# Tuned hybrid SSD/MLP kernel: halves of h on VectorE up to tile 6, other rows for the scalings of x, two sums ahead of row 5's weights, one warm-up product less

## Chip, cores and metric

One core of one Trainium2 chip. The metric is the time of one execution on the device in microseconds (us), taken as the median of several runs. A measurement of this kernel tells changes apart from about 0.2% on. Where single instructions are spoken of, their times come from one execution that the hardware profiler recorded, counted from its first instruction.

The engines have the profile's names: PE is TensorE (matrix products; PEld is its weight loads), DVE is VectorE, ACT is ScalarE, POOL is GpSimd, SP is SyncE, which issues most DMAs. An engine works through its own instructions in order; a "q" behind its name (SPq) stands for its sequencer.

## The reference, cut to what matters

One layer of a generator: a modulated RMS norm, one wide projection, a state-space scan and a gated MLP side by side, and an output projection. The change touches how the modulated, normed input `h` is made and fed to the first columns of the projection.

```python
shift, scale, gate = jnp.split(sc @ w_ada[l] + b_ada[l], 3, axis=-1)          # sc = silu(c), 2048
shift_c, scale_c, gate_c = jnp.split(scc @ w_ada[l] + b_ada[l], 3, axis=-1)   # scc = silu(c_ctx)
hc = _rmsnorm(ctx, g_pre[l]) * (1.0 + scale_c) + shift_c                      # 256 context tokens
zc = hc @ (w_in[l][:, :XBC_W + DT_W] if last else w_in[l])
...
hx = _rmsnorm(x, g_pre[l]) * (1.0 + scale[:, None]) + shift[:, None]          # 256 latent tokens
zx = hx @ w_in[l]
...
x = x + gate[:, None] * out
```

All is float32. The model width is 2048, there are 256 latent and 256 context tokens and one layer.

## The kernel before

**Layout.** The width of 2048 is cut into 16 tiles of 128, one per partition; tile k of `xT` holds 128 channels by 512 tokens. Columns 0 to 255 of a tile are one token group, 256 to 511 the other (the latent tokens), and each has its own scale and shift, two columns of `hab`.

**Products in two parts.** A float32 factor is split into a rounded part (`hi`, `hhi`) and the rest (`lo`, `hlo`), and a product of two float32 tiles is three products on PE: hi by hhi, hi by hlo, lo by hhi. ScalarE rounds the weights (`split_hi`, L376), VectorE subtracts (`split_lo`, L384; `split_dt`, L380, for 64 columns of the step sizes).

**Making h.** For tile k:
- `scale_x` (VectorE, L387): x times g_pre times the tokens' 1/rms, one operation of 512 columns.
- scale and shift of the tile, into `hab`: from 1 MB chunks of w_ada. For tiles 0 to 3 PE alone forms the sums (L224, L253). From tile 4 on tiles go in pairs; PE sums over twelve of sixteen parts of c (`ada_mm`, L253), VectorE over the other four in eight operations of 512 columns (`ada_part`, L262: "the sums" in this text), and `ada_fin` (VectorE: L268, transpose L275, L278) puts both together.
- `make_h` (ScalarE, L394): x times scale plus shift, twice, once rounded into `hhi` and once in full into `xT`, each in two halves of 256 columns; four instructions.
- `make_hl` (VectorE, L398): `hlo` = `xT` - `hhi`.

**Rows.** The first stage goes through the 16 tiles; step kt of it, "row kt" here, multiplies tile kt of h with the first seven tiles and the step-size columns of w_in (`wst[kt]`, 480 KB). Each row begins on PE with `psdt` (L446), then L466 and L467 for three tiles, `psdt` with hlo, L469, then L143 to L145 for the rest. Each row also carries the making of the next tile of h, n = kt + 1, on the other engines, and PE's share (L224, L253) of the scale and shift of later tiles.

**What sets the order.** It is written out by hand: `row_steps(kt)` returns a list of steps, and each engine gets its instructions in that order (`tc.manual_schedule`). Letters are steps: c, d, l split the weights of row n, h makes h, e makes hlo, x scales a tile of x (which ones in row kt: `XROW`), v is one of VectorE's sums, b and f finish a pair of scale and shift, a is PE's share of them, m, p, q, w are the products of row kt. The loads are issued by SyncE in program order, two chunks of w_ada and one tile of weights per row, into six buffers of 1 MB and three of 480 KB. They go through one queue and land in that order.

Ahead of row 0 the squares of x are summed by PE for the 1/rms (L341), with products of no use between them (`warm`, L319) that keep PE busy; 512 and 256 are their columns.

After the rows, from about 130 us on, the kernel goes through the rest of w_in and w_out in tiles of 1 MB, with the scan between; the change does not touch that.

Of the kernel before, what the change touches and what calls it, by code (L numbers as in the profile page):

```python
# [11 lines left out]
AF = mybir.ActivationFunctionType  # L12
ALU = mybir.AluOpType
# [15 lines left out]
NSING = 4  # L29
KD = 12  # L30

XROW = ((3, 4, 5), (6, 7, 8), (9,), (10, 11), (12, 13), (14, 15))

LAST = (-1, 4, 5, 0, 1, 2, 3, 6)

# [12 lines left out]
def tile_hybrid_ssd_mlp(  # L48
# [19 lines left out]
    nc = tc.nc  # L68
# [61 lines left out]
    hab = stp.tile([P, KT, 2, 2], F32, name="hab")  # L130
# [7 lines left out]
    hhi = [hpool.tile([P, TOK], F32R, name=f"hhi{k}") for k in range(KT)]  # L138
# [8 lines left out]
    def bc(ap, axis, n):  # L147
        u = ap.unsqueeze(axis)
        shp = list(u.shape)
        shp[axis] = n  # L150
        return u.to_broadcast(shp)
# [4 lines left out]
    def yseg(j):  # L156
        return y[:, j // 4, (j % 4) * 512 : (j % 4 + 1) * 512]
# [6 lines left out]
    zt, e = yseg(5)[:, 0:256], yseg(5)[:, 256:512]  # L164
# [12 lines left out]
    xT = stx.tile([P, KT, TOK], F32, name="xT")  # L177
# [78 lines left out]
    def ada_part(u, i):  # L256

        q, v = divmod(i, 2)
        if i == 0:
            part[u] = ada_raw.pop(4 * u - 2 * NSING), st2.tile([P, 4, 2], F32, tag="part", name=f"part{u}")  # L260
        raw, acc = part[u]
        nc.vector.scalar_tensor_tensor(cbj, raw[:, q * 512 : (q + 1) * 512], 1.0, cb[v], op0=ALU.mult, op1=ALU.mult,  # L262
                                       accum_out=acc[:, q, v : v + 1])
# [6 lines left out]
    def ada_fin(u):  # L270

        ps = ada_ps.pop(u)
        n = 64 * len(UNITS[u])
        tr = st2.tile([P, 128], F32, tag="row", name=f"adat{u}")
        nc.vector.transpose(tr[:, 0:n], ps[:, 0:n])  # L275
        m = UNITS[u][0]
        b = part.pop(u)[1] if u in part else bc(bab[:, m], 2, 2)
        nc.vector.tensor_tensor(hab[:, m : m + n // 64].rearrange("p k q v -> p (k q) v"),  # L278
                                tr[:, 0:n].rearrange("p (q r) -> p q r", r=32)[:, :, 0:2], b, op=ALU.add)
# [37 lines left out]
    def warm(*ns):  # L317
        for n in ns:
            nc.tensor.matmul(psw[:, 0:n], lhsT=ones, rhs=ones[:, 0:1].to_broadcast([P, n]), start=True, stop=True)  # L319
# [12 lines left out]
    for k in range(KT):  # L332
        sq = sqs[k % 7]
        if k % 2:
            nc.vector.tensor_tensor(sq, xT[:, k, :], xT[:, k, :], op=ALU.mult)
        else:
            nc.scalar.activation(sq, xT[:, k, :], AF.Square)
            if k == 0:
                nc.scalar.copy(cb[1], pcv[1])
        g = k % 4  # L340
        nc.tensor.matmul(pss[32 * g : 32 * g + 32, :], lhsT=ones[:, 0:32], rhs=sq, start=k < 4, stop=k >= KT - 4)  # L341
        if g == 3:
            warm(512)
            if k < 12:
                warm(256)

# [25 lines left out]
    def split_hi(kt, a=0, b=WST):  # L372
        if a == 0:
            sp0[kt] = (wp["spl"].tile([P, WST + 64], F32R, tag="hi", name=f"hi_st{kt}"),
                       wp["spl"].tile([P, WST - 64], F32R, tag="lo", name=f"lo_st{kt}"))
        nc.scalar.copy(sp0[kt][0][:, 64 + a : 64 + b], wraw[kt][:, a:b])  # L376

    def split_dt(kt):
        hi = sp0[kt][0]
        nc.vector.tensor_tensor(hi[:, 0:64], wraw[kt][:, 0:64], hi[:, 64:P].bitcast(F32), op=ALU.subtract)  # L380
# [5 lines left out]
    def scale_x(kt):  # L386
        nc.vector.scalar_tensor_tensor(xT[:, kt, :], xT[:, kt, :], pc[:, C_GPRE + kt : C_GPRE + kt + 1], rb,  # L387
                                       op0=ALU.mult, op1=ALU.mult)

    def make_h(kt):  # L390
        sl = (slice(256, 512), slice(0, 256))
        for t in (hhi[kt], xT[:, kt, :]):
            for v, s in enumerate(sl):
                nc.scalar.activation(t[:, s], xT[:, kt, s], AF.Identity, bias=hab[:, kt, 1, v : v + 1],  # L394
                                     scale=hab[:, kt, 0, v : v + 1])

    def make_hl(kt):
        nc.vector.tensor_tensor(hlo[kt], xT[:, kt, :], hhi[kt].bitcast(F32), op=ALU.subtract)  # L398

# [8 lines left out]
    def row_steps(kt):  # L408


        m = [("m", i) for i in range(-1, NST)]
        if kt == KT - 1:
            out_ = [("m", i) for i in LAST]
            out_.insert(3, ("t", 0))
            for i in range(2):
                out_.insert(out_.index(("m", 4 + i)) + 1, ("z", i))
            return out_
        n = kt + 1
        c_, d_, l_, h_, e_ = [(w, n) for w in ("c", "d", "l", "h", "e")]
        m0 = [("m", -1), ("p", 0), ("p", 1), ("p", 2), ("w", 0), ("q", 0), ("q", 1), ("q", 2)]  # L420
        m1 = [("m", i) for i in range(3, NST)]
        u = (n - NSING) // 2 + NSING
        x = [("x", k) for k in XROW[kt]] if kt < len(XROW) else []
        p = 4 * u - 2 * NSING
        if n < NSING:
            r = [("r", 2 * n), ("r", 2 * n + 1)]
            q = 8 if n == 1 else 6
            v = [("v", (NSING, i)) for i in range(4)] if n == NSING - 1 else []
            return (m0[:q] + r + [c_, ("k", n), d_, ("l1", n)] + m1[:1] + [("g", n), ("o", n), h_, ("l2", n)] + (v[:2] or x[:1])
                    + [e_] + v[2:] + (x if v else x[1:]) + m0[q:] + m1[1:])  # L430
        if kt % 2 == 0:
            v = [("v", (u + 1, i)) for i in range(4)] if n + 1 < KT else []
            return [e_, c_, d_, l_] + v + x + m0 + m1
        v = [("v", (u, i)) for i in range(4, 8)] + [("b", u)]
        a = [("a", c) for c in range(p + 1, p + 4)]
        t = v + [("f", u), h_, d_, l_, e_] + x + [("h", n + 1)]
        if n == NSING:
            return m0[:5] + a[:2] + m0[5:] + m1[:1] + a[2:] + [c_] + t + m1[1:]
        return a[:1] + m0 + a[1:] + [c_] + t + m1

    STEPS = {"a": ada_mm, "f": ada_fin, "v": lambda ui: ada_part(*ui), "b": ada_bias, "r": ada_rows, "x": scale_x, "e": make_hl, "k": ada_keep, "g": ada_sum, "o": ada_one,
             "h": make_h, "c": split_hi, "d": split_dt, "l": split_lo,
             "l1": lambda n: split_lo(n, 64, WH), "l2": lambda n: split_lo(n, WH)}

# [4 lines left out]
    def step(kt, what, i):  # L449
        if what in STEPS:  # L450
            STEPS[what](i)
        elif what == "z":
# [21 lines left out]

    split_hi(0, 0, WH)
    scale_x(0)
    ada_fin(0)
    split_dt(0)
    make_h(0)
    split_lo(0, 64, WH)  # L480
    make_hl(0)
    split_hi(0, WH)
    split_lo(0, WH)
# [469 lines left out]
    for n, i in enumerate(REST):  # L953
        lat = ORDER[i] >= 24
        ps = acp.tile([P, 256 if lat else 512], F32, tag="acc", name=f"psx{i}")
        for hf in range(2):
            whi, wlo = half(2 * n + hf)
            for kk in range(8):
                k = 8 * hf + kk
# [164 lines left out]
    for blk in range(16):  # L1124
# [11 lines left out]
        for u in range(8):  # L1136
            whi, wlo = half(base + blk * 8 + u)
            for kk in range(2):
                k = 2 * u + kk
                w = slice(kk * 512, (kk + 1) * 512)  # L1140
                for tk in range(2):
                    t = slice(256 + tk * P, 256 + (tk + 1) * P)
# [28 lines left out]
    op1 = ctx.enter_context(mkpool(name="op1", bufs=1))  # L1171
# [36 lines left out]
    for i in range(8):  # L1208
        tk, b = divmod(i, 4)
# [156 lines left out]
```

## Time and profile before

| | |
|---|---|
| median of 3 runs | 989.64 us (989.17 to 990.5) |
| profiled execution, its own time | 989.67 us |
| its span, first to last instruction | 987.9 us |
| mean granted clock of PE | 0.996 |
| PE busy | 977.2 us, 99% |
| VectorE busy | 651.2 us, 66% |
| ScalarE busy | 507.1 us, 51% |
| GpSimd busy | 112.5 us, 11% |
| DMA | 207.26 MB, 210 GB/s over the span; 420, 417 and 416 GB/s in the slices from 25 to 99 us |

How to read it: the span is what lies between the first and the last instruction; about 1.8 us of the execution's time lie around it. A busy PE is one that has a product under way, whatever its clock: the granted clock says at what share of full speed it ran. The lines of a timeline give the start and the duration in us, the engine, the line of the kernel, the operation, output and inputs by name, shape, how many were merged, and in brackets how long the engine had been idle before it and what ended that. Instructions of one engine overlap by some hundredths of a us at their ends, so durations add up to a little more than the time from start to start.

### The profile page before, as it was taken

Reading aid. Unit: us, or ns where it says so; the run is one execution under the profiler, and the core shown is the slowest. Engines: PE = TensorE matmul, PEld = TensorE weight load, DVE = VectorE, ACT = ScalarE, POOL = GpSimd, SP = SyncE. Lnnn points to the kernel's source line nnn. Section 1 sums busy time; section 2 is a strip of 40 time slices with the busy share of each in tenths; the row PEclk is TensorE's granted clock in tenths of the full one; section 3 lists DMA queues with packets and bytes.
Section 4 is the critical chain, followed back from the end, with each engine's and each line's share of the span. In section 5 each row is a group of like instructions: output and inputs, shape, how many; then the busy total and the mean of one; then the engine's idle time right before and its main releaser. Section 6 shows DMA issues by size and latency. Waiting matters only on the chain.

```text
span 987.9 us, 13636 instructions
## 1 busy us (share of the span) xinstructions
PE 977.2 (99%) x5312; PEld 787.8 (80%) x5312; DVE 651.2 (66%) x1029; ACT 507.1 (51%) x770; POOL 112.5 (11%) x162
## 2 busy tenths in 40 slices
PE   9999999999999999999999999999999999999997
PEld 3778888778887878787888888887888888888885
DVE  5687798868886566756667766767555564445636
ACT  4444458566665554545445343454565563346522
POOL 0000002432453122224000000000000000000000
PEclk9999999999999999999999999999999999999999
DMA  9999754233323424145878777774455445556722
GB/s 372 420 417 416 302 201 166 86 128 129 128 74 140 144 95 145 43 171 204 296 287 299 275 259 296 278 276 171 170 180 204 171 171 213 180 203 227 282 88 86
DMA packets 31985, 207.26 MB, mean 210 GB/s; under 512 B 4128, under 2 KB 4384, under 8 KB 8496
## 3 DMA queue, kind: packets, MB, share of 16 engines
q1 hardware_dynamic: 28800, 192.71, 52.2%
q0 software_dynamic: 2112, 12.65, 3.7%
q10 hardware_dynamic: 1008, 1.02, 0.3%
q8 instruction: 42, 0.69, 0.3%
q14 instruction: 23, 0.19, 0.1%
HBM read 204.20 MB, written 2.16 MB: 209 GB/s over the span
## 4 chain that ended last, share of the span: by engine, by line
PE 93%; DVE 3%; ACT 2%; DMA 2%; issue 0%; SPq 0%; ACTq 0%; DVEq 0%
PE pa L1143 12%; PE pa L1145 12%; PE pa L1144 12%; PE psx L143 9%; PE psx L145 8%; PE psx L144 8%; PE pm L1190 3%; PE pm L1192 3%; PE pm L1191 3%; PE pq L1192 2%; PE pq L1190 2%; PE pq L1191 2%; DMA wst<-in_wst_dram 2%; PE psc L813 1%; PE pso L866 1%; PE psada L253 1%
## 5 line engine op out<-in xcount | busy, mean ns | idle before, releaser
L88 DVE TENSOR_TENSOR lo_w<-w,hi_w 128x1024 fp32r<-128x1024 f32 x173 | 210.2, 1224 | 138.5 <-ACT hi_w L87 138.5
L87 ACT CAST hi_w<-w 128x1024 fp32r<-128x1024 f32 x173 | 182.1, 1052 | 203.6 <-PE pa L1145 132.4
L1143 PE MATMUL pa<-hi_w,hhi 128*128 128x512 f32 x512 | 202.3, 395 | 0.0
L1145 PE MATMUL pa<-hi_w,hlo 128*128 128x512 f32 x512 | 199.5, 390 | 0.0
L1144 PE MATMUL pa<-lo_w,hhi 128*128 128x512 f32 x512 | 199.3, 389 | 0.0
L143 PE MATMUL psx<-hhi,hi_w 128*128 128x512 f32 (+1 forms) x400 | 153.4, 383 | 0.0
L145 PE MATMUL psx<-hhi,lo_w 128*128 128x512 f32 (+1 forms) x400 | 145.9, 365 | 0.0
L144 PE MATMUL psx<-hlo,hi_w 128*128 128x512 f32 (+1 forms) x400 | 145.7, 364 | 0.0
L1143 PEld LDWEIGHTS pa<-hi_w,hhi 128*128 128x128 f32 x512 | 96.2, 188 | 20.7 <-issue 1.6
L1145 PEld LDWEIGHTS pa<-hi_w,hlo 128*128 128x128 f32 x512 | 96.1, 188 | 20.1
L1144 PEld LDWEIGHTS pa<-lo_w,hhi 128*128 128x128 f32 x512 | 96.2, 188 | 19.4 <-issue 0.2
L611 DVE SCALAR_TENSOR_TENSOR xbc<-psx,pc,xbc 128x248 f32<-128x248 f32 (+1 forms) x204 | 83.6, 473 | 34.8 <-ACT xbc L595 33.8
L536 DVE TENSOR_TENSOR lo_w<-w,hi_w 128x1024 fp32r<-128x1024 f32 x61 | 77.1, 1271 | 23.7 <-ACT hi_w L530 23.6
L143 PEld LDWEIGHTS psx<-hhi,hi_w 128*128 128x128 f32 x400 | 75.5, 189 | 13.4 <-issue 2.9
L145 PEld LDWEIGHTS psx<-hhi,lo_w 128*128 128x128 f32 x400 | 75.4, 189 | 12.5
L144 PEld LDWEIGHTS psx<-hlo,hi_w 128*128 128x128 f32 x400 | 75.6, 189 | 12.2 <-issue 1.7
L530 ACT CAST hi_w<-w 128x1024 fp32r<-128x1024 f32 x61 | 63.5, 1044 | 26.0 <-PE psx L144 12.9
L1001 DVE SCALAR_TENSOR_TENSOR junk<-gate,cb 128x2048 bf16<-128x2048 f32 x16 | 36.7, 2292 | 30.5 <-DMA gate<-in_wada_dram 30.5
L1190 PE MATMUL pm<-hi_w,hhi 128*128 128x512 f32 x128 | 49.9, 390 | 0.0
L1191 PE MATMUL pm<-lo_w,hhi 128*128 128x512 f32 x128 | 49.9, 390 | 0.0
L1192 PE MATMUL pm<-hi_w,hlo 128*128 128x512 f32 x128 | 49.6, 389 | 0.0
L765 ACT ACTIVATE R<-R,y 128x128 f32<-128x128 f32 x128 | 38.8, 391 | 0.0
(265 smaller groups left out, 1375.4 us busy)
## 6 DMA issues: line engine op xcount, KB each, us to landing
w<-in_wlat_dram SPq DMA_DIRECT2D x64, 1024.0 KB, 4.8
w<-in_wout_dram SPq DMA_DIRECT2D x32, 1024.0 KB, 4.8
ada<-in_wada_dram SPq DMA_DIRECT2D x30, 1024.0 KB, 12.5
w<-in_wxbc_dram SPq DMA_DIRECT2D x25, 1024.0 KB, 4.8
gate<-in_wada_dram SPq DMA_DIRECT2D x16, 1024.0 KB, 5.8
R<-acs POOLq DMA_DIRECT2D x8, 1024.0 KB, 5.1
wst<-in_wst_dram SPq DMA_DIRECT2D x15, 480.0 KB, 12.1
xT<-in_xch_dram SPq DMA_DIRECT2D x4, 1024.0 KB, 7.8
```

The lines of the kernel that those rows point to most:

```text
L87: nc.scalar.copy(hi, raw)
L88: nc.vector.tensor_tensor(lo, raw, hi.bitcast(F32), op=ALU.subtract)
L143: nc.tensor.matmul(ps, lhsT=whi, rhs=hhi[k][:, s], start=start, stop=False)
L144: nc.tensor.matmul(ps, lhsT=whi, rhs=hlo[k][:, s], start=False, stop=False)
L145: nc.tensor.matmul(ps, lhsT=wlo, rhs=hhi[k][:, s], start=False, stop=stop)
L611: nc.vector.scalar_tensor_tensor(ao, zi, cw[:, k : k + 1], ao, op0=ALU.mult, op1=ALU.add)
L1143: nc.tensor.matmul(pa[tk], lhsT=hhi[k][:, t], rhs=whi[:, w], start=k == 0, stop=False)
L1144: nc.tensor.matmul(pa[tk], lhsT=hhi[k][:, t], rhs=wlo[:, w], start=False, stop=False)
L1145: nc.tensor.matmul(pa[tk], lhsT=hlo[k][:, t], rhs=whi[:, w], start=False, stop=k == KT - 1)
L1190: nc.tensor.matmul(p, lhsT=yh[:, t], rhs=whi[:, w], start=j == 0, stop=False)
L1191: nc.tensor.matmul(p, lhsT=yh[:, t], rhs=wlo[:, w], start=False, stop=False)
L1192: nc.tensor.matmul(p, lhsT=yl[:, t], rhs=whi[:, w], start=False, stop=hf == 0 and j == 15)
```

## The change

Five edits, all in the first stage.

- `make_hs` is new: as `make_h`, but ScalarE makes columns 256 to 511 and VectorE columns 0 to 255, by a tensor_scalar with two operands per partition. It is used for tiles 0 to 3 and for tiles 4 and 6. The other tiles keep `make_h`.
- `XROW`: tiles of x are scaled in rows 0, 1, 3 and 5 rather than in rows 0 to 5. Even rows from 4 on no longer scale any.
- In the row that prepares row 5's weights, two of VectorE's eight sums stand ahead of the split of these weights.
- Ahead of row 0, `split_dt` goes before `ada_fin`.
- The warm-up product of 512 columns behind the third group of squares is left out.

```diff
--- before.py
+++ after.py
@@ -29,7 +29,7 @@
 NSING = 4
 KD = 12
 
-XROW = ((3, 4, 5), (6, 7, 8), (9,), (10, 11), (12, 13), (14, 15))
+XROW = ((3, 4, 5, 6), (7, 8, 9, 10, 11), (), (12, 13), (), (14, 15))
 
 LAST = (-1, 4, 5, 0, 1, 2, 3, 6)
 
@@ -340,7 +340,8 @@
         g = k % 4
         nc.tensor.matmul(pss[32 * g : 32 * g + 32, :], lhsT=ones[:, 0:32], rhs=sq, start=k < 4, stop=k >= KT - 4)
         if g == 3:
-            warm(512)
+            if k != 11:
+                warm(512)
             if k < 12:
                 warm(256)
 
@@ -393,6 +394,12 @@
             for v, s in enumerate(sl):
                 nc.scalar.activation(t[:, s], xT[:, kt, s], AF.Identity, bias=hab[:, kt, 1, v : v + 1],
                                      scale=hab[:, kt, 0, v : v + 1])
+
+    def make_hs(kt):
+        a, b = hab[:, kt, 0], hab[:, kt, 1]
+        for t in (hhi[kt], xT[:, kt, :]):
+            nc.scalar.activation(t[:, 256:512], xT[:, kt, 256:512], AF.Identity, bias=b[:, 0:1], scale=a[:, 0:1])
+            nc.vector.tensor_scalar(t[:, 0:256], xT[:, kt, 0:256], a[:, 1:2], b[:, 1:2], op0=ALU.mult, op1=ALU.add)
 
     def make_hl(kt):
         nc.vector.tensor_tensor(hlo[kt], xT[:, kt, :], hhi[kt].bitcast(F32), op=ALU.subtract)
@@ -426,19 +433,21 @@
             r = [("r", 2 * n), ("r", 2 * n + 1)]
             q = 8 if n == 1 else 6
             v = [("v", (NSING, i)) for i in range(4)] if n == NSING - 1 else []
-            return (m0[:q] + r + [c_, ("k", n), d_, ("l1", n)] + m1[:1] + [("g", n), ("o", n), h_, ("l2", n)] + (v[:2] or x[:1])
+            return (m0[:q] + r + [c_, ("k", n), d_, ("l1", n)] + m1[:1] + [("g", n), ("o", n), ("hs", n), ("l2", n)] + (v[:2] or x[:1])
                     + [e_] + v[2:] + (x if v else x[1:]) + m0[q:] + m1[1:])
         if kt % 2 == 0:
             v = [("v", (u + 1, i)) for i in range(4)] if n + 1 < KT else []
-            return [e_, c_, d_, l_] + v + x + m0 + m1
+            if n == NSING + 1:
+                return [e_, c_] + v[:2] + [d_, l_] + v[2:] + m0 + m1
+            return [e_, c_, d_, l_] + v + m0 + m1
         v = [("v", (u, i)) for i in range(4, 8)] + [("b", u)]
         a = [("a", c) for c in range(p + 1, p + 4)]
-        t = v + [("f", u), h_, d_, l_, e_] + x + [("h", n + 1)]
+        t = v + [("f", u), h_ if n > NSING + 2 else ("hs", n), d_, l_, e_] + x + [("h", n + 1)]
         if n == NSING:
             return m0[:5] + a[:2] + m0[5:] + m1[:1] + a[2:] + [c_] + t + m1[1:]
         return a[:1] + m0 + a[1:] + [c_] + t + m1
 
-    STEPS = {"a": ada_mm, "f": ada_fin, "v": lambda ui: ada_part(*ui), "b": ada_bias, "r": ada_rows, "x": scale_x, "e": make_hl, "k": ada_keep, "g": ada_sum, "o": ada_one,
+    STEPS = {"a": ada_mm, "f": ada_fin, "v": lambda ui: ada_part(*ui), "b": ada_bias, "r": ada_rows, "x": scale_x, "e": make_hl, "hs": make_hs, "k": ada_keep, "g": ada_sum, "o": ada_one,
              "h": make_h, "c": split_hi, "d": split_dt, "l": split_lo,
              "l1": lambda n: split_lo(n, 64, WH), "l2": lambda n: split_lo(n, WH)}
 
@@ -474,9 +483,9 @@
 
     split_hi(0, 0, WH)
     scale_x(0)
+    split_dt(0)
     ada_fin(0)
-    split_dt(0)
-    make_h(0)
+    make_hs(0)
     split_lo(0, 64, WH)
     make_hl(0)
     split_hi(0, WH)
```

How instructions move on VectorE, the engine that PE waits for at the start of row 6. First the place between tile 5's hlo (hlo_138) and row 6's split (wst_654 before, wst_655 now); wst_552 and wst_553 are row 5's weights, ada_548 and ada_549 the chunk of the sums for tiles 6 and 7. Before:

```order
L398 TENSOR_TENSOR hlo_138<-xT,hhi_122 128x512
L380 TENSOR_TENSOR hi_st_657<-wst_552,hi_st_657 128x64
L384 TENSOR_TENSOR lo_st_658<-wst_552,hi_st_657 128x896
L262 SCALAR_TENSOR_TENSOR y,part_662<-ada_548,y 128x512 x4
L387 SCALAR_TENSOR_TENSOR xT<-xT,pc,y 128x512 x2
L262 SCALAR_TENSOR_TENSOR y,part_662<-ada_548,y 128x512 x4
L268 TENSOR_TENSOR part_662<-part_662,bab 128x8
L275 STREAM_TRANSPOSE adat_766<-psada_698 128x128
L278 TENSOR_TENSOR hab<-adat_766,part_662 128x8
L380 TENSOR_TENSOR hi_st_758<-wst_654,hi_st_758 128x64
L384 TENSOR_TENSOR lo_st_759<-wst_654,hi_st_758 128x896
```

Now:

```order
L405 TENSOR_TENSOR hlo_138<-xT,hhi_122 128x512
L262 SCALAR_TENSOR_TENSOR y,part_661<-ada_549,y 128x512 x2
L381 TENSOR_TENSOR hi_st_658<-wst_553,hi_st_658 128x64
L385 TENSOR_TENSOR lo_st_659<-wst_553,hi_st_658 128x896
L262 SCALAR_TENSOR_TENSOR y,part_661<-ada_549,y 128x512 x6
L268 TENSOR_TENSOR part_661<-part_661,bab 128x8
L275 STREAM_TRANSPOSE adat_765<-psada_697 128x128
L278 TENSOR_TENSOR hab<-adat_765,part_661 128x8
L402 TENSOR_SCALAR hhi_123<-xT,hab 128x256
L402 TENSOR_SCALAR xT<-xT,hab 128x256
L381 TENSOR_TENSOR hi_st_757<-wst_655,hi_st_757 128x64
L385 TENSOR_TENSOR lo_st_758<-wst_655,hi_st_757 128x896
```

Two sums have moved ahead of row 5's split, the two scalings between the sums are gone, and two halves of tile 6's h stand ahead of row 6's split.

The second place is in row 2, where VectorE prepares row 3 and begins the sums for tiles 4 and 5 (ada_415); adac is the copy of PE's share of tile 3's scale and shift, hlo_136 is tile 3's. Before:

```order
L229 COPY adac_514<-psada_494 128x256
L380 TENSOR_TENSOR hi_st_511<-wst_413,hi_st_511 128x64
L384 TENSOR_TENSOR lo_st_512<-wst_413,hi_st_511 128x384
L384 TENSOR_TENSOR lo_st_512<-wst_413,hi_st_511 128x512
L262 SCALAR_TENSOR_TENSOR y,part_530<-ada_415,y 128x512 x2
L398 TENSOR_TENSOR hlo_136<-xT,hhi_120 128x512
L262 SCALAR_TENSOR_TENSOR y,part_530<-ada_415,y 128x512 x2
L387 SCALAR_TENSOR_TENSOR xT<-xT,pc,y 128x512
```

Now:

```order
L229 COPY adac_516<-psada_496 128x256
L381 TENSOR_TENSOR hi_st_513<-wst_413,hi_st_513 128x64
L385 TENSOR_TENSOR lo_st_514<-wst_413,hi_st_513 128x384
L402 TENSOR_SCALAR hhi_120<-xT,hab 128x256
L402 TENSOR_SCALAR xT<-xT,hab 128x256
L385 TENSOR_TENSOR lo_st_514<-wst_413,hi_st_513 128x512
L262 SCALAR_TENSOR_TENSOR y,part_532<-ada_415,y 128x512 x2
L405 TENSOR_TENSOR hlo_136<-xT,hhi_120 128x512
L262 SCALAR_TENSOR_TENSOR y,part_532<-ada_415,y 128x512 x6
```

Two halves of tile 3's h stand between the two parts of the split of row 3's weights, and the scaling between the sums is gone.

The third place is ahead of row 0: the scaling of tile 0, its scale and shift (adat, hab) and the first weights (wst_179). Before:

```order
L387 SCALAR_TENSOR_TENSOR xT<-xT,pc,y 128x512
L275 STREAM_TRANSPOSE adat_333<-psada_255 128x64
L278 TENSOR_TENSOR hab<-adat_333,bab 128x4
L380 TENSOR_TENSOR hi_st_329<-wst_179,hi_st_329 128x64
L384 TENSOR_TENSOR lo_st_330<-wst_179,hi_st_329 128x384
L398 TENSOR_TENSOR hlo_133<-xT,hhi_117 128x512
L384 TENSOR_TENSOR lo_st_330<-wst_179,hi_st_329 128x512
```

Now:

```order
L388 SCALAR_TENSOR_TENSOR xT<-xT,pc,y 128x512
L381 TENSOR_TENSOR hi_st_328<-wst_179,hi_st_328 128x64
L275 STREAM_TRANSPOSE adat_333<-psada_254 128x64
L278 TENSOR_TENSOR hab<-adat_333,bab 128x4
L402 TENSOR_SCALAR hhi_117<-xT,hab 128x256
L402 TENSOR_SCALAR xT<-xT,hab 128x256
L385 TENSOR_TENSOR lo_st_329<-wst_179,hi_st_328 128x384
L405 TENSOR_TENSOR hlo_133<-xT,hhi_117 128x512
L385 TENSOR_TENSOR lo_st_329<-wst_179,hi_st_328 128x512
```

The 64 step-size columns are split ahead of the transpose of tile 0's scale and shift, and two halves of tile 0's h come ahead of the larger split.

## The prediction

> **What bounds the kernel now.** I read four views, in this order: the waits of PE, then the timeline of PE around the longest of them, then the timelines of VectorE (DVE) and ScalarE (ACT) at that place, then the landings of the loads. PE is busy 99% of the span, so only what makes PE wait, or slows its clock, can be worth anything. Waits of PE, in us in total, times, longest:
>
> ```profile
> PE psdt L446 <- DVE lo_st L384: 2.2, 1, 2.2
> PE px L1284 <- ACT dg L1283: 1.5, 1, 1.5
> ```
>
> The second is at the end of the program, which the change leaves alone. The first is the start of row 6. Timeline of PE there (start, us, instruction, idle before and its releaser):
>
> ```profile
> 65.99 0.28 PE L145 MATMUL psx<-hhi,lo_st 128*128 128x256 f32 x1
> 68.48 0.50 PE L446 MATMUL psdt<-hhi,hi_st 128*128 128x512 f32 x1 [2.21 <-DVE lo_st L384]
> 69.28 0.63 PE L466 MATMUL psx<-hhi,hi_st 128*128 128x512 f32 x1
> 72.69 0.28 PE L143 MATMUL psx<-hhi,hi_st 128*128 128x256 f32 x1
> ```
>
> Row 5's last product is issued at 65.99; products of 256 columns follow each other by 0.12, so row 6 could have been issued at 66.11. It came at 68.48: **2.37 us**. Its products from 69.28 on take 0.63 where others take 0.39. Windows: the same stretch of a row (first product to the first L143) in row 4 and in row 6, then two pairs of rows; the column behind the engines is the granted clock, the last the DMA's GB/s:
>
> ```profile
> 53.27:56.02 2.75, 2.75 (x12) 2.10 (x12) 1.99 (x4) 2.75 (x6) 0.00 (x0) 1.00 1.00 402
> 68.48:72.69 4.21, 4.21 (x11) 3.31 (x12) 3.06 (x6) 3.78 (x7) 0.00 (x0) 0.59 1.01 418
> 75.89:88.44 12.55, 12.55 (x147) 10.30 (x143) 8.62 (x22) 5.94 (x10) 0.00 (x0) 1.00 1.02 415
> 88.44:101.00 12.56, 12.56 (x147) 10.29 (x143) 9.77 (x26) 6.00 (x11) 0.00 (x0) 1.00 1.02 418
> ```
>
> The wait of row 6 cost a second time: the granted clock fell to 0.59 of full in that stretch and it took 4.21 instead of 2.75, **1.46 us**. The loads run at 415 to 418 GB/s in every window, so their landings do not move however fast the engines are. That is what caps this change.
>
> What made row 6 late, VectorE first, then ScalarE:
>
> ```profile
> 56.21 0.69 DVE L398 TENSOR_TENSOR hlo<-xT,hhi 128x512 fp32r<-128x512 f32 x1
> 58.49 0.22 DVE L380 TENSOR_TENSOR hi_st<-wst,hi_st 128x64 fp32r<-128x64 f32 x1 [1.58 <-ACT hi_st L376]
> 58.63 1.08 DVE L384 TENSOR_TENSOR lo_st<-wst,hi_st 128x896 fp32r<-128x896 f32 x1
> 59.63 0.68 DVE L262 SCALAR_TENSOR_TENSOR y<-ada,y 128x512 f32<-128x512 f32 x1
> 62.45 1.41 DVE L387 SCALAR_TENSOR_TENSOR xT<-xT,pc,y 128x512 f32<-128x512 f32 x2
> 66.70 0.17 DVE L268 TENSOR_TENSOR part<-part,bab 128x8 f32<-128x8 f32 x1
> 66.78 0.31 DVE L275 STREAM_TRANSPOSE adat<-psada 128x128 f32<-128x128 f32 x1
> 67.35 1.09 DVE L384 TENSOR_TENSOR lo_st<-wst,hi_st 128x896 fp32r<-128x896 f32 x1
> ```
> ```profile
> 57.46 0.99 ACT L376 CAST hi_st<-wst 128x960 fp32r<-128x960 f32 x1 [1.28 <-DMA wst<-in_wst_dram]
> 63.62 1.00 ACT L376 CAST hi_st<-wst 128x960 fp32r<-128x960 f32 x1 [5.17 <-DMA wst<-in_wst_dram]
> 67.33 1.09 ACT L394 ACTIVATE hhi<-xT,hab 128x256 fp32r<-128x256 f32 x2 [2.71 <-DVE hab L278]
> 71.28 0.97 ACT L376 CAST hi_st<-wst 128x960 fp32r<-128x960 f32 x1
> ```
>
> Row 5's weights land at 57.4. VectorE had sat idle 1.58 us for them; then it splits them and works without a break through eight sums (L262), two scalings (L387) and ada_fin, and only at 67.33 does ScalarE get tile 6's scale and shift.
>
> **Row 5 to row 6, where the gain is made.** From 59.63 to 66.70 are 7.07 us: eight sums and two scalings. The scalings leave this stretch (62.45 to the next sum: 1.41 less the overlap of the last, about 1.34), so a sum with its accumulator read takes (7.07 - 1.34)/8 = 0.72. Two sums go ahead of L380, into the idle 1.58: 1.44 fits. Their chunk is loaded ahead of row 5's weights in the same queue, so it is there before 57.4. What is behind them: L380 and L384, hence row 5's L467 on PE. Left between L384 and L268 are six sums, 6 x 0.72 = 4.3: L268 at 63.9, 2.8 us earlier. The transpose behind it also needs PE's share of tiles 6 and 7:
>
> ```profile
> 62.02 1.95 PE L253 MATMUL psada<-ada,sc 128*32 128x128 f32 x64
> ```
>
> That ends at 63.97, as PE is no earlier in row 5 (below): just in time, at worst 0.1 late. ScalarE's half of tile 6 then starts at 67.33 - 2.8 = 64.55; row 6's cast (63.62, 1.00) ends at 64.62, so say 64.65. One half of 256 columns took 1.09/2 = 0.55: that half of hhi is there at 65.2.
>
> VectorE now makes the other halves itself, two tensor_scalar, ahead of L380 and L384. No row shows this with a rounded output; the nearest is
>
> ```profile
> L649 DVE TENSOR_SCALAR y<-y 128x256 f32<-128x256 f32 x1 | 0.3, 286 | 0.0
> ```
>
> 0.29 each. Bounds: from below the smallest VectorE operation above, 0.17; from above the two-tensor form, 0.22 for 64 columns (58.49) and 0.69 for 512 (56.21), so 0.42 for 256. I take 0.29, the same operation and size. So L384 of row 6 runs from 67.35 - 2.8 + 0.58 = 65.15 to 66.25, at the upper bound to 66.5. PE reads it in its third product; the fourth came 0.80 after the first (68.48, 69.28) and products of 512 follow each other by 0.23, so the third would start at 66.11 + 0.57 = 66.68. Hidden at either bound. **Row 6 starts at 66.1, PE never idles, the clock stays: 2.37 + 1.46 = 3.8 us on PE.**
>
> The Trainium skill, "TensorE: Matmul & The Clock Gate", section "Why this matters for your kernels", says to avoid PE idle gaps above about 3 us between bursts. By it a gap of 2.4 would leave the clock alone, PE's gain would be 2.37 alone, and the time 987.3. The 0.59 in the window of row 6 contradicts it, the measurement decides, and I leave it no chance worth counting.
>
> **The first rows bring nothing.** Row 0 and the warm-up:
>
> ```profile
> 14.61 1.56 PE L319 MATMUL psw<-ones 128*128 128x512 f32 x4
> 22.75 0.50 PE L446 MATMUL psdt<-hhi,hi_st 128*128 128x512 f32 x1 [0.35 <-ACT hhi L394]
> ```
>
> The removed product of 512 is about two thirds of 1.56 less its tail, 0.86, and the sums of squares behind it come 0.66 earlier at most (they then wait for the last square). Half a tile on ScalarE saves 0.55 against 1.09, split_dt ahead of ada_fin costs 0.15: row 0 starts about 1.05 earlier. But:
>
> ```profile
> 59.78 0.49 PE L467 MATMUL psx<-hhi,lo_st 128*128 128x512 f32 x1
> PEld psx L467 <- DVE lo_st L384: 0.3, 1, 0.3
> ```
>
> In row 5 PE already waits 0.3 for the split of weights that landed at 57.4 (cast to 58.45, L384 to 59.7). Whatever rows 0 to 4 win is lost there: worth 0. By the same wait, up to 0.3 that they lose is covered. For tiles 1 to 3 the halves on VectorE (0.58) wait for a scale from ScalarE, and behind them on VectorE stand the rest of the split, scalings or sums, and hlo, for which PE waits. Row 2, which makes tile 3, has one scaling less to pay for it (0.67, half of the 1.34 above), though behind that hlo. I cost this at nothing, bounds 0 to 0.3. The sixteen scalings stay sixteen; two more fall into row 1, behind hlo, where VectorE next waited
>
> ```profile
> 42.09 0.42 DVE L229 COPY adac<-psada 128x256 f32<-128x256 f32 x1 [1.69 <-PE psada L224]
> ```
>
> 1.69 for PE's share of tile 3: 1.34 fits, and without that cover the copy, and PE's products behind it, would be late by what overflows. Should the new short gaps of rows 0 to 4 lower the clock once, PE loses 1.46 less the 0.3, and keeps 2.6 of 3.8: 987.0, no other case.
>
> **What of 3.8 us survives.** From row 7 to row 14 a second chain runs as slowly as PE, and it has its own earliest start:
>
> ```profile
> 72.29 0.23 DVE L380 TENSOR_TENSOR hi_st<-wst,hi_st 128x64 fp32r<-128x64 f32 x1 [0.19 <-ACT hi_st L376]
> 79.30 0.17 DVE L268 TENSOR_TENSOR part<-part,bab 128x8 f32<-128x8 f32 x1
> 80.67 0.32 DVE L275 STREAM_TRANSPOSE adat<-psada 128x128 f32<-128x128 f32 x1 [1.21 <-PE psada L253]
> 93.29 0.31 DVE L275 STREAM_TRANSPOSE adat<-psada 128x128 f32<-128x128 f32 x1
> 121.93 0.19 PEld L446 LDWEIGHTS psdt<-hlo,hi_st 128*128 128x128 f32 x1 [0.21 <-DVE hlo L398]
> ```
>
> Row 7's cast stood at 71.28 behind tiles 6 and 7 on ScalarE. Now ScalarE is through with both at 64.65 + 2 x 0.55 + 4 x 0.5 = 67.75 (four halves in 2 us by the row at 67.33), and the cast waits for its weights instead. SyncE's issues of the weights of rows 7 and 9, each with its time to landing, and row 9's cast:
>
> ```profile
> 53.77 0.33 SPq L289 DMA_DIRECT2D wst<-in_wst_dram  x1
> DMA to landing us min/median/max: 15.9/15.9/15.9
> 72.35 0.33 SPq L289 DMA_DIRECT2D wst<-in_wst_dram  x1
> DMA to landing us min/median/max: 10.0/10.0/10.0
> 85.19 0.98 ACT L376 CAST hi_st<-wst 128x960 fp32r<-128x960 f32 x1
> ```
>
> Row 7's land at 53.77 + 15.9 = 69.7. The cast comes at 69.77, **1.5 us** earlier, not 3.8. Split and eight sums follow, so L268 moves from 79.30 to 77.8 and the transpose of tiles 8 and 9 to 77.9: it no longer waits for PE (which is at 80.6 - 3.8 = 76.8 there), and comes 80.67 - 77.9 = **2.77 us** earlier. From there one turn of the chain (scale and shift, ScalarE's four halves for two tiles, cast, split, eight sums, transpose) takes 93.29 - 80.67 = 12.62, PE's pair of rows 12.55. So the chain's 2.77 is what row 14 sees: at 121.93 PE already waits for hlo. PE's other microsecond goes into short waits in rows 8 to 14. Row 9's weights land at 72.35 + 10.0 = 82.35, its cast is due at 85.19 - 2.77 = 82.42: just there. Behind row 15 PE waits nowhere but at the end, by the table of waits, and loads there follow buffers that PE and VectorE free: 2.8 passes through.
>
> **Sum.** Against the profiled execution's 989.67 (span 987.9 and 1.8 around it; the median shown is 989.64, so no correction): 989.67 - 2.77 = **986.9**.
>
> **Rivals.**
> - *PE's gain carried whole*, 989.67 - 3.8 = 985.9: if weights of row 7 land earlier, or the chain gives way. For it: only 0.07 per pair separates chain and PE. Against: loads already run full. Chance 0.10.
> - *The loads bind earlier*: row 9's slack is 82.42 - 82.35, so every microsecond by which a landing of rows 7 to 13 is later than now is lost. Landings 1.3 later leave 1.5 of 2.8, about 988.2. For it: a full queue, and a change that issues at other times. Against: nothing is added to the queue ahead of these loads, and each was issued 10 to 16 us before it landed. Chance 0.22.
> - *Slower: the two sums block row 5's weights.* They stand ahead of L380 and L384. If VectorE gets to them after 57.05 (58.49 - 1.44), row 5 is late by the difference; it decides against the change from 3.8 later on, a start after 60.9, say by a chunk that lands late or the halves of tiles 3 and 4 costing more. At a start of 62.4 row 6 is 5.35 late: 989.67 + 1.5 = 991.2. Against: hlo ended at 56.9 and two scalings ahead of it stay as many. Chance 0.06.
>
> The Trainium skill, "DMA: Bandwidth & Descriptors", "Specifications", gives about 358 GB/s of HBM per core. By it a pair of rows would need 415 x 12.55/358 = 14.5 us (an estimate from the rows and that page), loads would bind in both kernels, and the time would stay at 989.7. The windows' 415 to 418 contradict it, so it gets no chance worth counting.
>
> **How the numbers follow.** Forecast 986.9 with 0.62 (its own range 986.4 to 987.5). The range 985.6 to 988.7 takes in the first two rivals and leaves the slower one and the far ends of the others out. Within 0.2%, about what a measurement of this kernel can tell from no change, is 987.7 to 991.6: nearly all of the second rival, 0.22; slower 0.06; faster 0.72.
>
> **What would show it.** Right: no wait of PE at 66, granted clock 1.00 from 66 to 75, the wait of L467 in row 5 still at 59.8 although row 0 starts near 21.7, row 7's cast waiting for DMA at 69.7, the transpose of tiles 8 and 9 near 77.9. Wrong: row 5 starting its split after 58.7, a clock below 1 in rows 0 to 5 from new short gaps, or casts of rows 9, 11, 13 waiting long for DMA.

## The result and the profile after

| | before | after |
|---|---|---|
| median | 989.13 us (988.16 to 990.5, 10 runs) | 987.15 us (986.84 to 987.54, 10 runs) |
| profiled execution, its own time | 989.67 us | 987.21 us |
| its span | 987.9 us | 985.5 us |

The ratio of the times is 0.9978, with a 95% interval of 0.9969 to 0.9988. The medians differ by 1.98 us, the two profiled executions by 2.46; the forecast was 2.77.

The waits of PE after (us in total, times, longest): the 2.2 us ahead of row 6 are gone, the one at the end of the program is as long as it was.

```profile
PE px L1293 <- ACT dg L1292: 1.5, 1, 1.5
PE psx L476 <- DVE lo_st L385: 0.2, 1, 0.2
```

The 0.2 us of L476 are new; they stand in row 4, at 54.74. The timeline of PE where the 2.2 us stood: row 5's last product, and row 6's first without a bracket, 0.12 behind it.

```profile
66.82 0.28 PE L145 MATMUL psx<-hhi,lo_st 128*128 128x256 f32 x1
66.94 0.40 PE L455 MATMUL psdt<-hhi,hi_st 128*128 128x512 f32 x1
```

Windows over the same part of row 6 as before, and over one pair of rows: 2.75 us instead of 4.21 at a granted clock of 1.00, loads at 415 to 422 GB/s.

```profile
66.94:69.69 2.75, 2.75 (x13) 1.99 (x12) 2.75 (x5) 1.72 (x4) 0.00 (x0) 1.00 1.04 422
75.37:87.90 12.53, 12.51 (x142) 10.00 (x141) 9.74 (x26) 5.93 (x10) 0.00 (x0) 1.00 1.02 415
```

The timeline of VectorE from the two moved sums to the transposes of tiles 6 and 7, 8 and 9, 10 and 11:

```profile
57.14 0.69 DVE L262 SCALAR_TENSOR_TENSOR y<-ada,y 128x512 f32<-128x512 f32 x1
57.87 0.69 DVE L262 SCALAR_TENSOR_TENSOR y<-ada,y 128x512 f32<-128x512 f32 x1
58.79 0.23 DVE L381 TENSOR_TENSOR hi_st<-wst,hi_st 128x64 fp32r<-128x64 f32 x1 [0.23 <-ACT hi_st L377]
...
64.33 0.17 DVE L268 TENSOR_TENSOR part<-part,bab 128x8 f32<-128x8 f32 x1
64.90 0.32 DVE L275 STREAM_TRANSPOSE adat<-psada 128x128 f32<-128x128 f32 x1 [0.40 <-PE psada L253]
65.45 0.41 DVE L402 TENSOR_SCALAR hhi<-xT,hab 128x256 fp32r<-128x256 f32 x1
...
78.20 0.31 DVE L275 STREAM_TRANSPOSE adat<-psada 128x128 f32<-128x128 f32 x1
90.81 0.31 DVE L275 STREAM_TRANSPOSE adat<-psada 128x128 f32<-128x128 f32 x1
```

The idle 1.58 us ahead of row 5's split has shrunk to 0.23: the two sums fill it. The transpose of tiles 8 and 9 comes at 78.20 and no longer waits for PE; before it was at 80.67, with 1.21 of waiting. That is 2.47 us earlier, as much as this pair of executions differs by (2.46). One turn of the chain later it is at 90.81, 12.61 behind, as before.

The casts of the weights of rows 5 and 7 on ScalarE:

```profile
57.76 0.99 ACT L377 CAST hi_st<-wst 128x960 fp32r<-128x960 f32 x1 [1.86 <-DMA wst<-in_wst_dram]
70.08 0.99 ACT L377 CAST hi_st<-wst 128x960 fp32r<-128x960 f32 x1 [1.42 <-DMA wst<-in_wst_dram]
```

Row 7's cast now waits for its weights, as predicted, but these land at 70.0 and not at 69.7, and row 5's 0.3 later too: in this execution the weights that the casts of the stage waited for came 0.2 to 0.3 later than in the one before.

### The profile page after: what moved, and what is told of

The parts are those of the page before. It is cut to its first block, busy times and chain, and to the rows that moved or that the text cites. A ratio compares the mean times of both kernels' runs of the same rounds, so it can differ in the third digit from the quotient of the medians.

```text
span 985.5 us, 13637 instructions
## 1 busy us (share of the span) xinstructions
PE 977.1 (99%) x5310; PEld 786.6 (80%) x5310; DVE 655.8 (67%) x1041; ACT 501.9 (51%) x758; POOL 112.5 (11%) x162
## 4 chain that ended last, share of the span: by engine, by line
PE 96%; DVE 1%; ACT 1%; issue 0%; ACTq 0%
PE pa L1152 12%; PE pa L1154 12%; PE pa L1153 12%; PE psx L143 9%; PE psx L145 9%; PE psx L144 9%; PE pm L1199 3%; PE pm L1201 3%; PE pm L1200 3%; PE pq L1201 2%; PE pq L1200 2%; PE pq L1199 2%; PE psada L253 2%; PE psc L822 1%; PE pso L875 1%; PE psw L319 1%
## 5 line engine op out<-in xcount | busy, mean ns | idle before, releaser
L377 ACT CAST hi_st<-wst 128x960 fp32r<-128x960 f32 (+2 forms) x17 | 16.0, 942 | 45.0 <-DMA wst<-in_wst_dram 45.0
```

## Experiments

One table holds the profiled executions of all runs that compute the full result. "Cast" is the start of row 7's cast, "transpose" that of tiles 8 and 9, "end of rows" the first product on `hi_w`, the first behind row 15. The last column is the execution's own time less "end of rows".

| kernel | own time | row 6 starts | PE's wait there | cast | transpose | end of rows | rest |
|---|---|---|---|---|---|---|---|
| before | 989.67 | 68.48 | 2.21 | 71.28 | 80.67 | 130.56 | 859.1 |
| before, 2nd profile | 990.06 | 68.91 | 2.21 | 71.72 | 81.10 | 131.00 | 859.1 |
| before, 3rd profile | 988.47 | 68.56 | 1.75 | 71.38 | 79.48 | 129.39 | 859.1 |
| before, gap filled | 988.45 | 68.53 | 0.49 | 71.34 | 79.46 | 129.33 | 859.1 |
| first rows alone | 988.61 | 68.50 | 1.31 | 71.31 | 79.41 | 129.27 | 859.3 |
| scalings alone | 987.80 | 67.19 | 0.99 | 70.00 | 78.10 | 128.01 | 859.8 |
| two sums alone | 987.19 | 67.34 | 0.76 | 70.16 | 78.26 | 128.15 | 859.0 |
| after | 987.21 | 66.94 | none | 70.08 | 78.20 | 128.14 | 859.1 |
| after without first rows | 989.63 | 66.34 | none | 69.79 | 77.91 | 127.83 | 861.8 |
| after, sums spread | 986.36 | 66.72 | none | 69.76 | 77.46 | 127.26 | 859.1 |
| the same without first rows | 987.51 | 66.28 | none | 69.96 | 77.04 | 127.42 | 860.1 |

### Without the first rows

Against after: the warm-up product is back, `ada_fin` is ahead of `split_dt`, and only tile 6 is halved.

```diff
-            if k != 11:
-                warm(512)
+            warm(512)
-            return (... ("hs", n), ("l2", n)] + ...
+            return (... h_, ("l2", n)] + ...
-        t = v + [("f", u), h_ if n > NSING + 2 else ("hs", n), d_, ...
+        t = v + [("f", u), ("hs", n) if n == NSING + 2 else h_, d_, ...
-    split_dt(0)
     ada_fin(0)
-    make_hs(0)
+    split_dt(0)
+    make_h(0)
```

> The changed kernel with the first rows put back as before: h of tiles 0 to 4 by ScalarE alone, the warm-up product and the order of split_dt as before. Left of the change: two sums ahead of row 5's weights, the moved scalings, the halves of tile 6. Theory (weights and the chain behind row 7's cast bound the gain): the same time as the changed kernel, 987.15 give or take 0.3, although row 5 starts on PE about 0.6 to 0.9 earlier than in the changed kernel (row 6 near 66.4 rather than 66.9) and L467 of row 5 waits again. Rival (the first rows carry part of the gain): 988 or more, nearer to the kernel before. Rival (PE's own time decides): 0.6 less than the changed kernel, 986.5.

Measured: 987.3 us (987.03 to 989.63, 11 runs) beside 989.02 for before, ratio 0.9988 (0.9979 to 0.9997). Eight of the eleven runs lie between 987.03 and 987.57, about where after lies. The other three are at 988.67, 989.6 (with a mean granted clock of 0.948, which was not followed) and 989.63, the profiled one. Row 6 starts 0.60 earlier than in after, and the rows end 0.31 earlier, no more than the 0.3 by which the loads landed earlier in this execution: cast to transpose is 8.12 in both. The profiled execution lost 2.7 us far behind the rows; the waits of PE that are there and not in after:

```profile
PE pa L1152 <- DVE lo_w L88: 1.4, 1, 1.4
PE ptm L1058 <- DVE vt L1118: 0.8, 1, 0.8
```

The first ends at 575 us, behind an operation of VectorE that waited for a load:

```profile
571.49 2.29 DVE L1009 SCALAR_TENSOR_TENSOR junk<-gate,cb 128x2048 bf16<-128x2048 f32 x1 [6.57 <-DMA gate<-in_wada_dram]
```

In after the same operation starts at 568.92. The "rest" of 859.8 and 860.1 in two other rows of the table goes with waits of PE at the same places (0.4 us up to 574 in the one, 0.8 up to 647 in the other). Why things are late there in some executions was not followed and stays open.

### The first rows alone

The edits that the run above took out, on before, without tile 6's halves.

> The kernel before with the edits of the first rows alone: halves of tiles 0 to 4 on VectorE, one warm-up product less, split_dt ahead of ada_fin. Theory: no gain from them, because row 5 waits for weights that land at 57.4 to 57.7 and row 6 for VectorE's chain behind them, which they don't touch: row 6 starts near 68.5 to 68.8 and the time is that of the kernel before, 989.1, or up to 0.7 less if the later end of row 5 shortens PE's gap so that the clock no longer falls. Rival (a gain at row 0 is carried): 988.1. Rival (halves cost PE 0.6 in row 3 and all of it is carried): 989.8.

Measured: 988.71 us (988.35 to 990.19, 11 runs) beside the same 989.02, ratio 0.9997 (0.9988 to 1.0005): no difference that can be measured. The cast is at 71.31, among those of the three profiles of before (71.28, 71.72 and 71.38). Row 5 starts at 60.20 (59.21, 59.66 and 59.83 in the three), so the edits bring row 5 later, not earlier; the wait at row 6 shrinks by that. Nine of the eleven runs lie below 989 us, against half of before's 28: the expectation allowed for a clock that falls less often behind a shorter gap, but these are too few runs to show it.

### The gap of before filled

Two products with zeros are added to `psdt` ahead of row 6, so that PE idles less there; nothing else is changed.

```diff
         elif i < 0:
+            if kt == NSING + 2:
+                for _ in range(2):
+                    nc.tensor.matmul(psdt, lhsT=ones, rhs=gate[:, 0:1].to_broadcast([P, TOK]), start=False, stop=False)
             dt_mm(kt, 0)
```

> The kernel before with two products by zeros added into psdt (512 columns each, float32, about 0.86 us each) at the place where PE waits ahead of row 6; nothing else moves, so the wait for VectorE stays and only the clock should be kept. Theory (the wait costs a second time through the clock, 1.46 on PE, and of that the chain behind row 7's cast lets through 1.2): granted clock 1.00 in rows 6 and 7, time 988.4 with a narrow spread, 0.7 to 1.2 below the kernel before. Rival (the clock after the gap costs nothing in the end): 989.1, the same as before. Rival (all of the gain of the change is the clock): 987.2.

Measured: 988.5 us (988.31 to 989.23, 11 runs), ratio 0.9993 (0.9984 to 1.0002). Row 6 starts where it did (68.53), yet the end of the rows comes 1.23 earlier than in the first profile of before. The 28 runs of before beside it fall into two groups, 14 from 988.37 to 988.87 and 14 from 989.17 to 990.07; the filled kernel lies in the lower one but for one run. So before can run in 988.4 as it stands, which the two profiles below took up.

### Before, profiled twice more

> The kernel before, unchanged, profiled once more: is the lowered clock at row 6 in all of its executions or in some? Theory (the clock falls in a part of the executions, by the phase in which the 2.4 us gap meets the gate): an execution that takes 988.3 to 988.9 us shows the granted clock at 1.00 from 62 to 80 us and row 7 starting near 74.5; one that takes 989.6 to 990.4 shows the clock near 0.6 for about 3.4 us from 68.5 and row 7 at about 75.9. Rival (the gap lowers the clock in every execution, and the two groups of times come from loads that land late near 550 or 650 us): the clock falls in both looks, row 7 is at 75.9 in both, and what they differ by appears after 500 us.

> A second execution of the unchanged kernel, with the same two expectations: by the theory the time tells whether the clock fell (under 989.0: it did not, row 7 near 74.5; over 989.5: it did, row 7 near 75.9); by the rival row 7 is at 75.9 whatever the time.

Measured: 990.06 and 988.47 us, one of each group. Windows over 70 to 74 us, and row 6's first product, in the execution of 990.06:

```profile
70.00:74.00 4.00, 4.00 (x14) 3.22 (x13) 3.81 (x7) 2.69 (x5) 0.00 (x0) 0.57 1.00 415
```
```profile
68.91 0.50 PE L446 MATMUL psdt<-hhi,hi_st 128*128 128x512 f32 x1 [2.21 <-DVE lo_st L384]
```

In that of 988.47:

```profile
70.00:74.00 4.00, 4.00 (x38) 3.16 (x41) 3.81 (x7) 2.35 (x4) 0.00 (x0) 1.00 1.01 417
```
```profile
68.56 0.50 PE L446 MATMUL psdt<-hhi,hi_st 128*128 128x512 f32 x1 [1.75 <-DVE lo_st L384]
```

The clock falls in one and not in the other: row 6's first product to row 7's takes 7.41 us in the one and 5.96 in the other. (The counts 14 and 38 do not compare: the 38 hold short products of L253, which the first window does not reach.) The transposes of tiles 8 and 9, first in the execution of 990.06, then in that of 988.47:

```profile
81.10 0.32 DVE L275 STREAM_TRANSPOSE adat<-psada 128x128 f32<-128x128 f32 x1 [1.21 <-PE psada L253]
```
```profile
79.48 0.31 DVE L275 STREAM_TRANSPOSE adat<-psada 128x128 f32<-128x128 f32 x1
```

The two executions are 1.59 apart in their own time and 1.61 at the end of the rows. Of this, 0.34 is there already in row 7's cast, and 1.28 comes between the cast and the transpose, which waits for PE only where the clock fell. So a fall of the clock costs this kernel about 1.3 us.

It does not make the whole upper group. Of the 26 runs of before above 989 us in the two sets measured beside the experiments (28 and 22 runs), 18 have a mean granted clock of 0.996 or 0.997, as the two profiled executions in which it fell (0.996 and 0.997); the other 8 have 0.998 or 0.999, as all 24 runs below 989 us. None of the 8 was profiled, and a loss far behind the rows, the rival of the expectation, is open for them.

What decides whether the clock falls is not shown: the expectation spoke of a phase, but PE was idle 2.21 in both executions in which the clock fell, and 1.75, 1.31 and 0.49 in three in which it did not, so the length of the gap sorts them as well.

### Each of the two parts that count, alone

The scalings moved, on before; and the two sums ahead of row 5's split, on before.

```diff
-XROW = ((3, 4, 5), (6, 7, 8), (9,), (10, 11), (12, 13), (14, 15))
+XROW = ((3, 4, 5, 6), (7, 8, 9, 10, 11), (), (12, 13), (), (14, 15))
...
-            return [e_, c_, d_, l_] + v + x + m0 + m1
+            return [e_, c_, d_, l_] + v + m0 + m1
```
```diff
+            if n == NSING + 1:
+                return [e_, c_] + v[:2] + [d_, l_] + v[2:] + x + m0 + m1
             return [e_, c_, d_, l_] + v + x + m0 + m1
```

> The kernel before with the moved scalings alone (no sums ahead of row 5's weights, no halves on VectorE, first rows as before). Theory: VectorE's stretch between row 5's split and ada_fin gets 1.34 shorter; PE waits about 1 us for hhi of tile 6 (row 6 near 67.1), the clock holds, row 7's cast comes at its landing or 0.3 behind it, so nearly the whole gain of the change is there: 987.2 to 987.5. Rival (gains of the two parts add up): 988.1. Rival (still a gap above which the clock falls): 988.5.

> The kernel before with two sums ahead of row 5's weights alone (scalings where they were). Theory: as with the scalings alone, 1.44 less between row 5's split and ada_fin: row 6 near 67.0, row 7's cast at 69.9, 987.1 to 987.4: either part is enough, because row 7's weights land at 69.7 in any case. Rival (gains add up): 988.1. Rival (the sums hold up row 5's split): no better than 988.4.

Measured: the scalings alone 987.45 us (987.21 to 988.18, 10 runs) beside 989.64 for before, ratio 0.9981 (0.9972 to 0.999); the sums alone 987.31 (986.94 to 987.97, 9 runs), ratio 0.9979 (0.997 to 0.9988). Either part alone comes within 0.3 us of after's 987.15, which was measured beside another set of runs of before. Row 6 in each, first the scalings, then the sums:

```profile
67.19 0.50 PE L452 MATMUL psdt<-hhi,hi_st 128*128 128x512 f32 x1 [0.99 <-DVE lo_st L384]
```
```profile
67.34 0.50 PE L448 MATMUL psdt<-hhi,hi_st 128*128 128x512 f32 x1 [0.76 <-DVE lo_st L384]
```

Each leaves a wait, at a granted clock that stays at 1.00, and PE later than in after. But row 7's cast stands at 70.00 and 70.16, as in after (70.08), so the rest follows as in after. The cast has no bracket in either: with one part alone ScalarE, and not the load, is the last thing it waits for. The second part buys PE time that the chain does not pass on.

### The chain given room

If the chain from row 7's weights is what caps the gain, moving sums into VectorE's idle time behind row 7 must bring more. On after: two of eight sums ahead of row 7's split, and from row 9 on one sum ahead of the hlo of the odd tile.

```diff
-            return [e_, c_, d_, l_] + v + m0 + m1
+            if n == NSING + 3:
+                return [e_, c_] + v[:2] + [d_, l_] + v[2:] + m0 + m1
+            return v[:1] + [e_, c_, d_, l_] + v[1:] + m0 + m1
```

> The changed kernel with VectorE's idle stretches of rows 6 to 14 used for sums: in row 6 two of the eight sums ahead of the split of row 7's weights, from row 8 on one sum ahead of the hlo of the odd tile, where VectorE sat idle 1.28 us. Theory (the chain from row 7's weights through VectorE and ScalarE binds, 0.5 us behind PE): the transpose of tiles 8 and 9 comes 0.7 to 1.1 us earlier, no more waits of PE for hhi and hlo in rows 8 to 14, and the time is that of PE alone, 0.5 below the changed kernel: 986.65. Rival (loads bind from row 7 on): the same as the changed kernel, 987.15. Rival (sums ahead of the splits hold up rows 7 and 9): slower, 987.5 or more.

Measured: 986.41 us (986.34 to 986.61, 6 runs) beside 989.02, ratio 0.9972 (0.996 to 0.9983): the fastest kernel of the study, 0.74 below after's median. VectorE in it:

```profile
71.04 0.22 DVE L381 TENSOR_TENSOR hi_st<-wst,hi_st 128x64 fp32r<-128x64 f32 x1
76.57 0.17 DVE L268 TENSOR_TENSOR part<-part,bab 128x8 f32<-128x8 f32 x1
77.46 0.32 DVE L275 STREAM_TRANSPOSE adat<-psada 128x128 f32<-128x128 f32 x1 [0.73 <-PE psada L253]
```

L268 is 1.55 ahead of its place in after (78.12), and the transpose waits for PE again, 0.73: now PE is the later of the two, which it was not in after. Some of this is the landing: the cast stands at 69.76, 0.32 ahead of after's. Against the run without the first rows, whose cast is at 69.79, the rows end 0.57 earlier, about the 0.5 that was expected.

The same change without the first rows:

> The kernel with sums in VectorE's idle stretches of rows 6 to 14, with the first rows put back as before (h of tiles 0 to 4 by ScalarE alone, warm-up and split_dt as before). Theory: with the chain out of the way PE's own lead counts, and without the halves of tiles 3 and 4 row 7 starts 0.4 earlier (72.3 against 72.7); so now the first rows' edits cost 0.4: 986.0. Rival (they cost nothing, row 5's weights take it all): 986.4. Rival (loads bind next): 986.4 or more with casts waiting for DMA in front of idle PE.

Measured: 987.0 us (985.96 to 988.0, 7 runs) beside 989.64, ratio 0.9973 (0.9962 to 0.9984). Its best run is the lowest of the study, but the runs spread over 2 us, and the profiled one lost 1.0 behind the rows, most of it up to 647 us. From its cast to the end of the rows it takes 57.46 us, against 57.50 with the first rows. Whether the first rows pay once the chain has room is not settled.

### What a half on VectorE costs

Tiles 1 to 3 get their halves with two constants, with one operand per partition and one constant, and with one operand alone; tiles 0, 4 and 6 as in after. So the context tokens' halves of h (columns 0 to 255; the expectation calls them the latent ones) lack their shift or scale in tiles 1 to 3, and the run stands in no table.

```diff
-            nc.vector.tensor_scalar(t[:, 0:256], xT[:, kt, 0:256], a[:, 1:2], b[:, 1:2], op0=ALU.mult, op1=ALU.add)
+            s1, s2 = ((1.0, 0.5), (a[:, 1:2], 0.5), (a[:, 1:2], None))[kt - 1] if kt in (1, 2, 3) else (a[:, 1:2], b[:, 1:2])
...
```

> The changed kernel, but VectorE's halves use other operands: tile 1 multiplies and adds constants, tile 2 multiplies by the scale of each partition and adds a constant, tile 3 only multiplies by the scale (so the latent halves of h of tiles 1 to 3 lack their shift or scale); tiles 0, 4 and 6 as in the changed kernel, 0.41 us for 256 columns. Theory (two operands per partition cost the fast form): tile 1 0.29 as L649 before, tile 2 and 3 between 0.29 and 0.41, by which the operand is told. Rival (place and neighbours make it slow, ScalarE reading the same tile): 0.41 in all. Time 987.2 in any case.

Measured, in the timeline of VectorE (one execution; its own time is 987.04 us):

```profile
22.07 0.41 DVE L406 TENSOR_SCALAR hhi<-xT,hab 128x256 fp32r<-128x256 f32 x1
29.47 0.29 DVE L406 TENSOR_SCALAR hhi<-xT 128x256 fp32r<-128x256 f32 x1
36.09 0.35 DVE L406 TENSOR_SCALAR hhi<-xT,hab 128x256 fp32r<-128x256 f32 x1 [0.36 <-ACT hab L241]
43.47 0.35 DVE L404 TENSOR_SCALAR hhi<-xT,hab 128x256 fp32r<-128x256 f32 x1 [0.40 <-ACT hab L241]
```

Two constants take 0.29, one operand per partition 0.35 with or without a constant beside it, two 0.41: about 0.06 for each operand read per partition.

## Why the prediction held, and where its steps did not

**The cap was right.** The prediction's main step was that 3.8 us go on PE but the chain that starts at row 7's weights lets only part of it through. In all seven full runs that left the chain as it is and in which the clock did not fall, the transpose comes 8.10 to 8.12 behind row 7's cast, the end of the rows 57.96 to 58.06 behind it, whether row 6 starts at 66.34 or at 68.56. Giving the chain room brought more; either of two parts that each left PE a wait brought nearly as much as both.

**The gain is of two kinds, and the sum did not tell them apart.** The 2.77 was 1.51 by which the cast moves and 1.21 by which the transpose had waited for PE, with 0.05 of rounding. The second is there in the two profiles in which the clock fell and not in the third. Against that third profile of before, after gains 1.30 in the cast and 1.26 in its own time; against the first 2.46. The step that failed is "the median shown is 989.64, so no correction": before's median falls between two groups and depends on how many runs of each it holds (989.02, 989.13, 989.64) and, as counted above, on long runs whose mean clock shows no fall. After has no gap there and its runs lie within 0.7 us. The gain in the medians, 1.98, is a mixture of the two.

**Landings.** The forecast put row 7's landing at 69.7; it came at 70.0 in after's execution, and 2.77 - 0.30 = 2.47 is what the transpose gained. In the run without the first rows and in the one with the sums spread the cast came at 69.79 and 69.76, as forecast. So this term moves with the execution, and loads that land late are the second rival's mechanism, at a quarter of its price. The prediction had the loads at 415 to 418 GB/s in every window; its first window, in row 4, has 402.

**The first rows: worth nothing, for another reason than given.** I had row 0 start near 21.7 and lose its gain to row 5's weights, with losses covered up to 0.3. The cover was misread: 0.3 is the wait of a weight load (PEld). On PE the product behind L467 of row 5 came 0.33 later (59.78 to 60.11) where 0.23 is usual, so 0.1 could be covered. Row 0 started at 22.91. The first six warm-up products, the same in both kernels, before and then after:

```profile
1.12 4.46 PE L319 MATMUL psw<-ones 128*128 128x512 f32 x6 [1.12 <-DVE ones L113]
```
```profile
1.12 5.49 PE L319 MATMUL psw<-ones 128*128 128x512 f32 x6 [1.12 <-DVE ones L113]
```

They took 1.03 more, about the whole of the expected 1.05. That is chance, not the change: in the other two profiles of before they took 4.94 and 5.14. From their end to row 0 it is 17.17 in before and 16.30 in after, 16.02 with the sums spread: the gain was there, 0.87 to 1.15. Then it was lost, and more. Each half took 0.41 and not 0.29 (the upper bound was 0.42), and in rows 1 and 2 VectorE stood waiting 0.55 for the scale that the half of tiles 2 and 3 needs. Tile 3's half and its hlo:

```profile
43.97 0.41 DVE L402 TENSOR_SCALAR hhi<-xT,hab 128x256 fp32r<-128x256 f32 x1 [0.55 <-ACT hab L241]
...
46.70 0.69 DVE L405 TENSOR_TENSOR hlo<-xT,hhi 128x512 fp32r<-128x512 f32 x1
```

Tile 3's hlo came at 46.70 instead of 45.77. From row 0 to row 5 are 36.40 to 36.46 in the three profiles of before, 37.20 in after and 37.99 with the sums spread; with the cheaper halves of the last experiment they are 36.78. Row 5 started at 60.11 instead of 59.21, 0.9 late where I had allowed 0.3, and the wait of L467 in row 5 that was to stay at 59.8 is gone. None of it reached the end, not because row 5 waits for its weights but because the chain binds behind it: after's row 7 stands at 72.89, and the spread version shows that PE's share of tiles 8 and 9 is ready at 77.46 with row 7 at 72.68, so at about 77.67 in after, 0.5 ahead of the transpose at 78.20. By this reckoning another 0.5 us lost in the first rows would have been free too, and more not. The prediction had not counted on this slack: that the loss cost nothing was luck.

**Row 6.** It started at 66.94, not 66.1, because row 5's last product came 0.83 later. The sums fitted: behind them VectorE still stood 0.23 for row 5's cast, so the slower rival did not even begin. L268 was forecast at 63.9 and came at 64.33, the 0.3 of the late landing and 0.1 more; behind it the transpose waited 0.40 for PE, where I had allowed 0.1.

**The clock.** The step that priced its fall was right in size: from row 6's to row 7's first product are 7.41 us in the execution of 990.06 and 5.96 in that of 988.47, 1.45 against the predicted 1.46. It was wrong as a fixed property of the kernel, and of the 1.45 the chain hands on 1.28.

## What to carry to other kernels

- Where two chains run at the same pace, a gain on one counts only up to the earliest start of the other: look for what that start waits for (here the landing of one load), take the smaller gain, and then give the second chain room.
- Before a wait is priced from one profile, look at a second execution: a wait long enough to lower the clock in some executions costs twice in those alone, and the times then fall into groups whose median means little.
- Moving half of an operation to a second engine moves its wait for the operands too, and holds up all that stands behind it there.

## What was not expected of the hardware

- A gap of 2.21 us on PE was followed by half the granted clock in two profiles of the unchanged kernel, one of 1.75 was not in a third. Windows show the clock at 0.50 from 69.27 to 72.67 in the first and from 70.24 to 73.65 in the second: 3.4 us in both, beginning 0.8 and 1.3 us after the end of the gap. The Trainium skill, "TensorE: Matmul & The Clock Gate", "What's actually happening", describes a free-running window of activity of about 3.4 us and half clock after an idle one, with a phase that differs from run to run. The length agrees with the 3.4 here. A gap shorter than the window is not said there to be enough; here it was, twice. The two different delays would fit such a phase; no run here shows it.
- The first six products of a program took 4.46 us in the first profile of before, 4.94 in the second and 5.49 in after, with a granted clock of 1.00 in the windows over them: the column does not show this slowness. The same section says that the number of slow products at a start varies with the phase; the spread of 1.03 would fit that.
- An operand read per partition costs a tensor_scalar of 128 x 256 float32 about 0.06 us each (0.29, 0.35 and 0.41 with none, one and two, in one execution).
